# Low query parts laid out twice for the attention scores, and the meta keys' value block padded to 128 rows

## Chip, cores and metric

The kernel runs on one core of a Trainium2 chip. The metric is device time in microseconds (us) of one execution of the whole program; lower is better. In the profile PE is TensorE's matmuls, PEld its weight loads, DVE is VectorE, ACT is ScalarE, POOL is GpSimd and SP the queue that issues most DMAs.

## What is computed

One decoder layer. 16 learned meta tokens stand ahead of 1024 input tokens, so attention has 1040 key positions. Reduced to what matters here:

```python
hn = rms_norm(h, norm1_gain);  proj = hn @ w_in             # q, k, v and the conv input
q, k = rms_norm(q), rms_norm(k)                             # 4 heads x 2 components x 64
q, k = apply_partial_rope(q), apply_partial_rope(k)
s = einsum('bqhcd,bkhcd->bhcqk', q, k) * scale              # two score maps per head
p = softmax(where(mask, s, -inf))                           # causal
a = p[:, :, 0] - lam * p[:, :, 1]                           # differential attention
o = einsum('bhqk,bkhe->bqhe', a, v)                         # value width 128
h = h + concat(rms_norm(o) * 0.8, conv_branch(u)) @ w_out
h = h + relu(rms_norm(h) @ w_up) ** 2 @ w_down
return h[:, 16:]
```

Model width is 1024, feed-forward width 4096, everything float32.

## The kernel before, in words

Float32 products are made from two-part numbers: a high part that TensorE's reduced float32 format (fp32r) holds exactly, and a low part, the rest. The helper `split` (lines 119 to 121) makes both: ScalarE copies to the high part (L120), VectorE, or GpSimd on request, subtracts it for the low part (L121). A product is then high x high + high x low + low x high, the three matmuls of `three` (L311 to L313).

The stages follow one another: norm and transposes of x, projections for the conv branch, k, q and v (to about 285 us, the last ones mixed with the first attention work), attention with the conv half and part of the attention half of the output projection set in between (to about 506 us), the rest of the projection with the second norm, and the feed-forward part (from about 540 us).

Attention goes over 32 units (i, h): query tile i from 7 down to 0, head h from 0 to 3. Tile i sees 16 + 128 (i + 1) keys, so units get smaller. For each unit:

- `qstack` (L496 to L513) lays out the 128 queries of head h: for both components c a high part of 64 columns, written twice side by side (`qt_dup`, by ScalarE at L503, by VectorE at L505 for i of 0 and 1), and a low part written once (`qt_lo`, L506; by VectorE for i above 3, by GpSimd for i up to 3). Three 128x128 transposes (L510) turn it into a PSUM bank, and one ScalarE copy (L512) brings it to the tile `uq`, whose ring has 3 buffers (UQB). In `uq` slots 0 and 1 have the high part of component c on all 128 rows (twice 64); slot 2 has the low part of component 0 on rows 0 to 63 and that of component 1 on rows 64 to 127.
- `scores` (L515 to L583) multiplies with the keys. The key tile `kst` has for each component the high part of k on one half of the 128 rows and the low part on the other half; the order of the halves is such that the high part of component c lies on rows 64c to 64c + 63. Line L532 contracts 128 rows, high q with high and low k; line L533 adds low q with high k, and contracts 64 rows. A causal mask is added to the last 128 columns by a bf16 matmul (L535). A unit's keys come in one or two pieces of at most 512 columns per component; for i = 7 the 16 meta keys are a piece of their own, in the fourth part of the query bank.
- The rest of `scores` takes a row maximum on VectorE (L572 or L542) and the exponential with its sum on ScalarE (L576 or L546); score tiles have two buffers.
- `mix` (L585 to L605) combines the two components on VectorE (L591), transposes the result in blocks of 128 keys, four to a PSUM bank (L602), and splits it into `u` (L120, L121). Block 0 is the 16 meta keys; where the number of blocks is one more than a multiple of four (i = 7 and 3) it has a bank of its own, 16 rows high.
- `values` (L607 to L621) multiplies `u` with the values, two matmuls per block (L616, L617). For block 0 both contract 16 rows, with the tile `vm` (16 rows) as the other operand.

Query layouts are issued three units ahead of `mix`, scores two ahead (LOOK). Values follow one unit behind. At given units the output projection's matmuls (`po`, from `conv_out` and `attn_out`) are put in at another priority. All instructions of an engine run in an order fixed at build time: `TileContext` is told to lay it out by priorities and a planner's own estimate of durations, so an edit can move the order of work that it doesn't touch. The PSUM ring `x` (2 banks) is shared by query transposes, `values` and `po`.

Of the kernel before, what the change touches and what calls it, by code (L numbers as in the profile page):

```python
# [9 lines left out]
F32 = mybir.dt.float32  # L10
F32R = mybir.dt.float32r
BF16 = mybir.dt.bfloat16
AF = mybir.ActivationFunctionType
# [3 lines left out]
P = 128  # L17
# [12 lines left out]
LOOK = 2  # L30
UQB = 3
FIN = 3
# [21 lines left out]
def hybrid_layer_kernel(  # L54
# [40 lines left out]
    RS = G  # L95
# [1 line left out]
    warm = cp.tile([P, 1], F32, tag="warm", name="warm")  # L97
# [14 lines left out]
    def rsqrt_of(dst, ss, eps):  # L112
        """dst = (ss + eps) ** -0.5"""
        parts, n = ss.shape
        ms = small([P, 8], "ms", 4)[:parts, :n]
        RS.tensor_scalar(ms, ss, eps, None, ALU.add)
        G.tensor_tensor(out=dst, in0=ms, in1=mhalf[:parts, :n], op=ALU.pow)
# [32 lines left out]

# [1 line left out]
    # the meta tokens: high parts in columns 0..15, low parts in columns 32..47  # L152
    xm = cp.tile([P, 8, 48], F32R, tag="xm", name="xm")
# [16 lines left out]
    def norm_tile(src, parts, dst, t=-1):  # L170
        """src [parts, D] -> src * rstd * norm1, transposed and split by dst(half, bank)."""
        ss = small([P, 1], "ss")
        junk = sp.tile([P, D], BF16, tag="tmp", name="junk", bufs=4)
        S.activation(junk[:parts, :], src, AF.Square, accum_out=ss[:parts])
        rs = small([P, 1], "rs")
        rsqrt_of(rs[:parts], ss[:parts], D * EPS)
        V.tensor_scalar(src, src, rs[:parts, 0:1], D ** 0.5, ALU.mult, ALU.mult)
        for hf in range(2):
            bank = pa.tile([P, 4, P], F32, tag="mm", name="xtr") if t in XPA else tr_bank("xtr")
            for q in range(4):  # L180
                k = hf * 4 + q
                T.transpose(bank[:, q, :parts], src[:, k * P:(k + 1) * P], ident[:parts, :parts])
            dst(hf, bank)
# [26 lines left out]

    # small parameters
    cvec = cp.tile([P, 4, 4], F32, tag="cvec", name="cvec")
# [43 lines left out]

# [1 line left out]
    NK = NPOS // 2  # L258
# [7 lines left out]
    def fir(dst, src, k0, tap, n, bias, ka, kb):  # L266
        """dst[k - k0] = bias + sum_d tap(d) src[k - d], k = ka .. kb - 1"""
        if bias is None:
            S.activation(dst[:, ka - k0:kb - k0], src[:, ka:kb], AF.Copy, scale=tap(0))
        else:  # L270
            S.activation(dst[:, ka - k0:kb - k0], src[:, ka:kb], AF.Identity, bias=bias, scale=tap(0))
        for d in range(1, n):
            lo = max(ka, d)
            o = dst[:, lo - k0:kb - k0]
            V.scalar_tensor_tensor(o, src[:, lo - d:kb - d], tap(d), o, ALU.mult, ALU.add)
# [3 lines left out]
    def conv_taps(j, ka, kb, which):  # L279
        """31 taps as three filters of half the length: on the even, the odd and the summed positions."""  # L280
        hb = yt[:, j, :].rearrange("p (s k) -> p s k", s=2)
# [27 lines left out]
    def three(ps, st, mv, first, last):  # L309
        """ps += st_hi*mv_hi + st_hi*mv_lo + st_lo*mv_hi"""  # L310
        T.matmul(ps, st[0], mv[0], start=first, stop=False)  # L311
        T.matmul(ps, st[0], mv[1], start=False, stop=False)  # L312
        T.matmul(ps, st[1], mv[0], start=False, stop=last)  # L313
# [27 lines left out]

# [1 line left out]
    def proj(w, t, bank=None):  # L343
        """tokens of tile t (None: meta) times the 512 columns of w."""
        if bank is None:
            bank = pa.tile([P, 512], F32, tag="mm", name="pq")
        if t is None:
            # rows 0..15: the high parts of the meta tokens, rows 32..47: the low parts
            for k in range(8):
                wk = w[k // 4]  # L350
                for part in range(2):
                    T.matmul(bank[:48, :], xm[:, k, :], wk[:, part, k % 4, :],
                             start=k == 0 and part == 0, stop=k == 7 and part == 1)
            both = tmp([P, 512], F32, "pm")[:NMETA, :]
            S.activation(both, bank[32:32 + NMETA, :], AF.Copy)
            V.tensor_tensor(out=both, in0=both, in1=bank[:NMETA, :], op=ALU.add)
            return both
        for k in range(8):
            c0 = xcol(t)
            st = (xT[t // 2][:, 0, k, c0:c0 + P], xT[t // 2][:, 1, k, c0:c0 + P])  # L360
            wk = w[k // 4]
            three(bank, st, (wk[:, 0, k % 4, :], wk[:, 1, k % 4, :]), k == 0, k == 7)
        return bank
# [8 lines left out]
    def rope_inplace(v, tab, tt, n):  # L372
        """v [n, 8, 64]: rotates the first 16 of each 64."""
        m1 = tmp([P, 2, 8, 2, 8], F32, "rot")
# [76 lines left out]
    def conv_norm(t):  # L451
        """layer norm over the channels of tile t, token-major, in place of the conv output"""
        cs = slice(t * P, (t + 1) * P)
# [37 lines left out]

# [1 line left out]
    ma = [None, None]  # L493
    l0s = small([P, NT, NH], "l0s", bufs=1)

    def qstack(i, h, pool=None):  # L496
        qt = sp.tile([P, 384], F32R, tag="raw", name="qt", bufs=4)
        qsrc = qs[:, i, h * P:(h + 1) * P].rearrange("p (c d) -> p c d", c=2)
        qt_dup = qt[:, 0:256].rearrange("p (c b d) -> p c b d", c=2, b=2)
        qt_lo = qt[:, 256:384].rearrange("p (c d) -> p c d", c=2)  # L500
        qdup = qsrc.unsqueeze(2).broadcast_to([P, 2, 2, HD])
        if i > QDI:
            S.activation(qt_dup, qdup, AF.Copy)  # L503
        else:
            V.tensor_copy(qt_dup, qdup)  # L505
        (G if i <= QG else V).tensor_tensor(out=qt_lo, in0=qsrc, in1=qt_dup[:, :, 0, :].bitcast(F32), op=ALU.subtract)  # L506
        qtf = qt.bitcast(F32)
        bank = pb.tile([P, 4, P], F32, tag="x", name="qtr", bufs=2)
        for q in range(3):
            T.transpose(bank[:, q, :], qtf[:, q * P:(q + 1) * P], ident)  # L510
        uq = pool.tile([P, 3, P], F32R, tag=f"uq{h}", name=f"uq{h}") if pool else ap.tile([P, 3, P], F32R, tag="uq", name="uq", bufs=UQB)
        S.activation(uq, bank[:, 0:3, :], AF.Copy)  # L512
        return uq, bank  # L513

    def scores(i, h, uq, bank, pool=None):  # L515
# [12 lines left out]
        def score(ps, c, k0, k1):  # L528
            kt = kst[h // 2][:, 2 * (h % 2) + c, :]
            rows = slice(64 * c, 64 * c + 64)  # L530
            diag = k1 == nkeys
            T.matmul(ps, uq[:, c, :], kt[:, k0:k1], start=True, stop=False)  # L532
            T.matmul(ps, uq[rows, 2, :], kt[rows, k0:k1], start=False, stop=not diag)  # L533
            if diag:
                T.matmul(ps[:, k1 - k0 - P:k1 - k0], identb, maskb, start=False, stop=True)  # L535
# [49 lines left out]
    def mix(i, h, pt, l1):  # L585
# [7 lines left out]
        u = ap.tile([P, 2, 9, P], F32R, tag="u", name="u")  # L593
        merged = (i + 2) % 4 != 1
        groups = [list(range(b, min(b + 4, i + 2))) for b in range(0 if merged else 1, i + 2, 4)]
        for grp in groups if merged else [[0]] + groups:
            bank = tr_bank("atr")
            n = P if merged or grp[0] else NMETA
            for q, b in enumerate(grp):
                # of block 0 only the first NMETA keys are used  # L600
                k0 = NMETA + P * (b - 1) if b else 0
                T.transpose(bank[:n, q, :], a[:, k0:k0 + n], ident)  # L602
            b0, b1 = grp[0], grp[-1] + 1
            split(u[:n, 0, b0:b1, :], u[:n, 1, b0:b1, :], bank[:n, :b1 - b0, :])
        return u  # L605

    def values(i, h, u):  # L607
# [5 lines left out]
        for b in range(i + 2):  # L613
            n = P if b else NMETA
            vb = (vs[(b - 1) // 4][:, (b - 1) % 4] if b else vm)[:, h]
            T.matmul(ops, u[:n, 0, b, :], vb.rearrange("p a e -> p (a e)"), start=b == 0, stop=False)  # L616
            T.matmul(ops[:, 0:P], u[:n, 1, b, :], vb[:, 0, :], start=False, stop=b == i + 1)  # L617
        ob = ap.tile([P, P], F32, tag="ob", name="ob")
# [23 lines left out]

# [1 line left out]
    def wout(e, nh, rows):  # L644
# [64 lines left out]
    ap = at_pool.__enter__()  # L709
    vm = ap.tile([NMETA, NH, 2, P], F32R, tag="vm", name="vm", bufs=1)  # L710
    split(vm[:, :, 0, :], vm[:, :, 1, :], psm.rearrange("p (h e) -> p h e", h=NH))

# [57 lines left out]

# [1 line left out]
    hn = [None, None]  # L772
# [30 lines left out]

# [1 line left out]
    NB = NF // 512  # L805
# [97 lines left out]
```

## Time and profile before

| | |
|---|---|
| median of 3 runs | 1240.09 us |
| lowest and highest | 1232.40 and 1240.16 us |
| span of the profiled execution | 1236.3 us |
| median less span | 3.8 us |
| TensorE busy, share of the span | 99% |
| weight loads busy | 81% |
| VectorE busy | 55% |
| ScalarE busy | 36% |
| GpSimd busy | 10% |

The time of the profiled execution is not listed apart from its span. The span runs from the first to the last instruction; what lies around it is taken as the 3.8 us that the median is longer. TensorE's busy time is made of modelled ends: consecutive matmuls overlap in it, so the distance from one matmul's start to the next one's tells more than its duration.

### The profile page before, as it was taken

To read this page: it belongs to the slowest core of one execution; us is meant where nothing else is said; L and a number is where in the kernel's file an instruction comes from. 1 tells how busy PE (TensorE), PEld (TensorE's weight loads), DVE (VectorE), ACT (ScalarE), POOL (GpSimd) and SP (SyncE) were. 2 spreads that over 40 slices of the span, in tenths; PEclk is the share of its full clock that TensorE was granted. 3 is DMA by queue.
4 is the path that set the end of the run, shared out by engine and by line. 5 is a ranking of instruction groups with operands and counts; after the bars stand their busy time and mean duration, and the time that the engine had idled before them with its cause. 6 is when DMAs were issued, how large, how long until landed. Compare 5 with 4: busy or idle time off the path is not lost.

```text
span 1236.3 us, 15700 instructions
## 1 busy us (share of the span) xinstructions
PE 1220.1 (99%) x6048; PEld 1002.1 (81%) x6048; DVE 677.3 (55%) x1286; ACT 439.1 (36%) x1120; POOL 126.2 (10%) x143
## 2 busy tenths in 40 slices
PE   6999999999999999999999999999999999999998
PEld 6999888766777777888888888888888888888887
DVE  7699899767676667674244334324324343342322
ACT  7422556265565655653033022122221230230310
POOL 3000853130011311210000000000000000000000
PEclk9999999989999999999999999999999999999999
DMA  7320110001122401421022012102202210220112
GB/s 260 95 69 1 35 35 11 25 17 52 51 86 72 140 28 31 136 74 44 25 68 68 8 61 68 51 19 68 69 1 68 68 39 30 69 68 1 34 43 94
DMA packets 37979, 70.64 MB, mean 57 GB/s; under 512 B 4864, under 2 KB 5120, under 8 KB 37904
## 3 DMA queue, kind: packets, MB, share of 16 engines
q1 hardware_dynamic: 37904, 69.64, 17.5%
q8 instruction: 47, 0.77, 0.3%
q14 instruction: 28, 0.23, 0.1%
HBM read 61.23 MB, written 8.39 MB: 56 GB/s over the span
## 4 chain that ended last, share of the span: by engine, by line
PE 96%; issue 2%; DVE 1%; POOL 1%; DMA 0%; ACT 0%; SPq 0%; POOLq 0%; DVEq 0%
PE pf L311 9%; PE pf L312 9%; PE pd L313 9%; PE pf L313 9%; PE pd L312 9%; PE pd L311 9%; PE ops L616 3%; PE sps L533 3%; PE pu L311 3%; PE pu L313 2%; PE pu L312 2%; PE po L311 2%; PE pq L312 2%; PE pq L311 2%; PE pq L313 2%; PE po L313 2%
## 5 line engine op out<-in xcount | busy, mean ns | idle before, releaser
L846 DVE TENSOR_TENSOR h<-h,pd 128x512 f32<-128x512 f32 x128 | 87.9, 687 | 205.5 <-PE pd L313 205.5
L312 PE MATMUL pf<-hn,wup 128*128 128x512 f32 x512 | 199.5, 390 | 0.0
L311 PE MATMUL pd<-wdn,at 128*128 128x512 f32 x512 | 199.2, 389 | 0.0
L312 PE MATMUL pd<-wdn,at 128*128 128x512 f32 x512 | 199.2, 389 | 0.0
L313 PE MATMUL pd<-wdn,at 128*128 128x512 f32 x512 | 199.2, 389 | 0.0
L313 PE MATMUL pf<-hn,wup 128*128 128x512 f32 x512 | 199.1, 389 | 0.0
L311 PE MATMUL pf<-hn,wup 128*128 128x512 f32 x512 | 198.4, 390 | 0.7 <-ACT hn L120 0.7
L831 DVE TENSOR_TENSOR r<-r 128x512 f32<-128x512 f32 x64 | 44.3, 691 | 162.9 <-ACT r L830 162.9
L120 ACT ACTIVATE wdn<-raw 128x512 fp32r<-128x512 f32 x64 | 37.8, 626 | 268.0 <-PE pd L313 246.8
L311 PEld LDWEIGHTS pf<-hn,wup 128*128 128x128 f32 x512 | 96.0, 188 | 20.8 <-ACT hn L120 1.0
L312 PEld LDWEIGHTS pd<-wdn,at 128*128 128x128 f32 x512 | 96.1, 188 | 20.0
L311 PEld LDWEIGHTS pd<-wdn,at 128*128 128x128 f32 x512 | 96.1, 188 | 19.9
L313 PEld LDWEIGHTS pd<-wdn,at 128*128 128x128 f32 x512 | 96.1, 188 | 19.9
L313 PEld LDWEIGHTS pf<-hn,wup 128*128 128x128 f32 x512 | 96.1, 188 | 19.8
L312 PEld LDWEIGHTS pf<-hn,wup 128*128 128x128 f32 x512 | 96.1, 188 | 19.8
L830 ACT ACTIVATE r<-pf 128x512 f32<-128x512 f32 x64 | 38.2, 597 | 169.8 <-PE pf L313 169.0
L312 PE MATMUL pu<-xT,w 128*128 128x260 f32 x256 | 72.2, 285 | 0.0
L313 PE MATMUL pu<-xT,w 128*128 128x260 f32 x256 | 71.5, 284 | 0.0
L311 PE MATMUL pu<-xT,w 128*128 128x260 f32 x256 | 71.5, 285 | 0.0
L121 DVE TENSOR_TENSOR at<-r,at 128x512 fp32r<-128x512 f32 x64 | 44.3, 692 | 37.8 <-ACT at L120 37.7
L120 ACT ACTIVATE at<-r 128x512 fp32r<-128x512 f32 x64 | 40.3, 630 | 41.6 <-DVE r L831 41.6
L131 DVE SCALAR_TENSOR_TENSOR wup<-raw,gains,wup 128x512 fp32r<-128x512 f32 x64 | 45.3, 748 | 15.6 <-ACT wup L130 14.5
(218 smaller groups left out, 2227.8 us busy)
## 6 DMA issues: line engine op xcount, KB each, us to landing
raw<-in_w_up SPq DMA_DIRECT2D x64, 256.0 KB, 3.3
raw<-in_w_down SPq DMA_DIRECT2D x64, 256.0 KB, 3.0
raw<-in_w_in SPq DMA_DIRECT2D x40, 256.0 KB, 2.9
xs<-in_x SPq DMA_DIRECT2D x8, 512.0 KB, 6.5
raw<-in_w_out SPq DMA_DIRECT2D x16, 256.0 KB, 2.9
xr<-in_x SPq DMA_DIRECT2D x16, 256.0 KB, 2.7
cvo<-cvo SPq DMA_DIRECT2D x16, 256.0 KB, 2.1
h<-cvo SPq DMA_DIRECT2D x16, 256.0 KB, 5.2
```

The costliest lines, as they stand in the source:

```text
L120: S.activation(hi, src, AF.Copy)
L121: (eng or V).tensor_tensor(out=lo, in0=src, in1=hi.bitcast(F32), op=ALU.subtract)
L131: V.scalar_tensor_tensor(w[:, 1, k, :], raw, g, w[:, 0, k, :].bitcast(F32), ALU.mult, ALU.subtract)
L311: T.matmul(ps, st[0], mv[0], start=first, stop=False)
L312: T.matmul(ps, st[0], mv[1], start=False, stop=False)
L313: T.matmul(ps, st[1], mv[0], start=False, stop=last)
L533: T.matmul(ps, uq[rows, 2, :], kt[rows, k0:k1], start=False, stop=not diag)
L616: T.matmul(ops, u[:n, 0, b, :], vb.rearrange("p a e -> p (a e)"), start=b == 0, stop=False)
L830: S.activation(r, ps, AF.Relu)
L831: V.tensor_tensor(out=r, in0=r, in1=r, op=ALU.mult)
L846: V.tensor_tensor(out=hs, in0=hs, in1=ps, op=ALU.add)
```

## The change

The low part of the queries is written twice too, like the high part. `uq` gets four slots in place of three: slot 2 + c has the low part of component c on all 128 rows. Line L533 then contracts 128 rows: low q with high and low k, which adds the product low x low that was left out before. A query layout has four transposes, its low part and its copy are wider, and the ring of `uq` has two buffers.

The tile `vm` gets 128 rows, cleared by a GpSimd memset; the meta values stay in rows 0 to 15. Block 0 of `mix` is transposed and split at full height everywhere, so that its rows 16 to 127 hold other keys' weights, which meet the zero rows of `vm`. The partly filled bank of `mix` comes first in place of last, so for i = 5 the groups are 3 and 4 blocks (before 4 and 3), and for i = 4 they are 2 and 4 (before 4 and 2).

```diff
-UQB = 3
+UQB = 2
...
     def qstack(i, h, pool=None):
-        qt = sp.tile([P, 384], F32R, tag="raw", name="qt", bufs=4)
+        qt = sp.tile([P, 2, 2, 2, HD], F32R, tag="raw", name="qt", bufs=4)
...
-        qt_dup = qt[:, 0:256].rearrange("p (c b d) -> p c b d", c=2, b=2)
-        qt_lo = qt[:, 256:384].rearrange("p (c d) -> p c d", c=2)
+        qt_dup, qt_lo = qt[:, 0], qt[:, 1]
...
-        (G if i <= QG else V).tensor_tensor(out=qt_lo, in0=qsrc, in1=qt_dup[:, :, 0, :].bitcast(F32), op=ALU.subtract)
-        qtf = qt.bitcast(F32)
+        (G if i <= QG else V).tensor_tensor(out=qt_lo, in0=qdup, in1=qt_dup.bitcast(F32), op=ALU.subtract)
+        qtf = qt.bitcast(F32).rearrange("p a c b d -> p (a c b d)")
...
-        for q in range(3):
+        for q in range(4):
             T.transpose(bank[:, q, :], qtf[:, q * P:(q + 1) * P], ident)
-        uq = pool.tile([P, 3, P], F32R, tag=f"uq{h}", name=f"uq{h}") if pool else ap.tile([P, 3, P], F32R, tag="uq", name="uq", bufs=UQB)
-        S.activation(uq, bank[:, 0:3, :], AF.Copy)
+        uq = pool.tile([P, 4, P], F32R, tag=f"uq{h}", name=f"uq{h}") if pool else ap.tile([P, 4, P], F32R, tag="uq", name="uq", bufs=UQB)
+        S.activation(uq, bank, AF.Copy)
...
-            T.matmul(ps, uq[rows, 2, :], kt[rows, k0:k1], start=False, stop=not diag)
+            T.matmul(ps, uq[:, 2 + c, :], kt[:, k0:k1], start=False, stop=not diag)
...
-        merged = (i + 2) % 4 != 1
-        groups = [list(range(b, min(b + 4, i + 2))) for b in range(0 if merged else 1, i + 2, 4)]
-        for grp in groups if merged else [[0]] + groups:
+        first = (i + 2) % 4 or 4
+        groups = [list(range(first))] + [list(range(b, b + 4)) for b in range(first, i + 2, 4)]
+        for grp in groups:
...
-                T.transpose(bank[:n, q, :], a[:, k0:k0 + n], ident)
+                T.transpose(bank[:, q, :], a[:, k0:k0 + P], ident)
             b0, b1 = grp[0], grp[-1] + 1
-            split(u[:n, 0, b0:b1, :], u[:n, 1, b0:b1, :], bank[:n, :b1 - b0, :])
+            split(u[:, 0, b0:b1, :], u[:, 1, b0:b1, :], bank[:, :b1 - b0, :])
...
-            n = P if b else NMETA
             vb = (vs[(b - 1) // 4][:, (b - 1) % 4] if b else vm)[:, h]
-            T.matmul(ops, u[:n, 0, b, :], vb.rearrange("p a e -> p (a e)"), start=b == 0, stop=False)
-            T.matmul(ops[:, 0:P], u[:n, 1, b, :], vb[:, 0, :], start=False, stop=b == i + 1)
+            T.matmul(ops, u[:, 0, b, :], vb.rearrange("p a e -> p (a e)"), start=b == 0, stop=False)
+            T.matmul(ops[:, 0:P], u[:, 1, b, :], vb[:, 0, :], start=False, stop=b == i + 1)
...
-    vm = ap.tile([NMETA, NH, 2, P], F32R, tag="vm", name="vm", bufs=1)
-    split(vm[:, :, 0, :], vm[:, :, 1, :], psm.rearrange("p (h e) -> p h e", h=NH))
+    vm = ap.tile([P, NH, 2, P], F32R, tag="vm", name="vm", bufs=1)
+    G.memset(vm.bitcast(F32), 0.0)
+    split(vm[:NMETA, :, 0, :], vm[:NMETA, :, 1, :], psm.rearrange("p (h e) -> p h e", h=NH))
```

The rest of the diff takes out comments.

## Rows read from the trace of the kernel before

**Rows 1.** Busy time by stretch: us (xinstructions) per engine, granted clock, DMA share, GB/s.

```profile
...
285.00:300.00 15.00, 14.20 (x69) 9.60 (x66) 11.54 (x28) 10.24 (x23) 0.00 (x0) 1.00 0.22 70
285.00:506.00 221.00, 219.82 (x1192) 164.74 (x1190) 152.61 (x382) 128.49 (x355) 33.34 (x42) 0.99 0.20 65
540.00:1236.00 696.00, 692.67 (x3069) 573.33 (x3067) 258.98 (x386) 156.63 (x257) 0.79 (x2) 1.00 0.16 50
...
```

**Rows 2.** The view of cores: span and mean granted TensorE clock.

```profile
...
core 0: 1236.3 us, clock 0.996
...
```

**Rows 3.** Timeline from 315.8 us: start us, us, engine, line, tiles, form [idle before].

```profile
...
315.85 0.49 ACT L512 ACTIVATE uq<-qtr 128x384 fp32r<-128x384 f32 x1
...
316.27 0.18 PEld L533 LDWEIGHTS sps<-kst,uq 64*128 64x128 f32 x1 [0.22 <-issue]
...
316.68 0.23 PE L535 MATMUL sps<-maskb,identb 128*128 128x128 bf16 x1
...
316.84 0.38 PE L616 MATMUL ops<-vm,u 16*128 16x256 f32 x1
...
317.06 0.22 PE L617 MATMUL ops<-vm,u 16*128 16x128 f32 x1
...
317.21 0.39 PE L616 MATMUL ops<-vs,u 128*128 128x256 f32 x1
...
317.43 0.19 PEld L616 LDWEIGHTS ops<-vs,u 128*128 128x128 f32 x1
317.49 0.33 PE L616 MATMUL ops<-vs,u 128*128 128x256 f32 x1
...
317.72 0.33 PE L616 MATMUL ops<-vs,u 128*128 128x256 f32 x1
...
318.18 0.42 PE L532 MATMUL sps<-kst,uq 128*128 128x456 f32 x1
...
318.53 0.47 PE L533 MATMUL sps<-kst,uq 64*128 64x456 f32 x1
...
318.93 0.48 PE L532 MATMUL sps<-kst,uq 128*128 128x456 f32 x1
...
319.34 0.47 PE L533 MATMUL sps<-kst,uq 64*128 64x456 f32 x1
...
319.74 0.23 PE L535 MATMUL sps<-maskb,identb 128*128 128x128 bf16 x1
...
319.77 0.36 PE L616 MATMUL ops<-vs,u 128*128 128x256 f32 x1
...
```

**Rows 4.** The score tile's view: L533's matmuls, and its engine's idle time.

```profile
...
L533 PE MATMUL sps<-kst,uq x104: 330/438/792, 245.9 to 495.7; 64*128 64x512 f32 x16, 64*128 64x456 f32 x16, 64*128 64x392 f32 x16, 64*128 64x328 f32 x16
...
  issue: 23.0, 105
...
```

**Rows 5.** Timeline from 433.3 us: the end of unit (3, 2)'s scores.

```profile
...
433.30 0.39 PE L532 MATMUL sps<-kst,uq 128*128 128x264 f32 x1
...
433.62 0.38 PE L533 MATMUL sps<-kst,uq 64*128 64x264 f32 x1
...
433.93 0.23 PE L535 MATMUL sps<-maskb,identb 128*128 128x128 bf16 x1
...
```

**Rows 6.** Timeline of TensorE at 278.2 us: eight 128x128 transposes.

```profile
...
278.22 1.03 PE L480 MATMUL ctr<-ident,yt 128*128 128x128 f32 x8
...
```

**Rows 7.** Groups by line and form: busy us, mean ns | idle before, releaser.

```profile
...
L506 DVE TENSOR_TENSOR qt<-qs,qt 128x128 fp32r<-128x128 f32 x16 | 5.6, 349 | 1.7 <-ACT qt L503 1.7
...
L512 ACT ACTIVATE uq<-qtr 128x384 fp32r<-128x384 f32 x32 | 15.7, 489 | 21.3 <-PE qtr L510 21.2
...
L506 POOL TENSOR_TENSOR qt<-qs,qt 128x128 fp32r<-128x128 f32 x16 | 8.4, 527 | 32.0 <-DVE qt L505 22.4 <-ACT qt L503 9.6
L154 POOL MEMSET xm<- 128x384 f32 x1 | 0.4, 418 | 0.0
...
```

**Rows 8.** Timeline at 439.1 us: the query copy of unit (2, 0).

```profile
...
439.13 0.49 ACT L512 ACTIVATE uq<-qtr 128x384 fp32r<-128x384 f32 x1 [0.97 <-PE qtr L510]
...
```

More of the change, by code (lines that the diff above doesn't have):

```diff
@@ L529, in score @@
             kt = kst[h // 2][:, 2 * (h % 2) + c, :]
-            rows = slice(64 * c, 64 * c + 64)
             diag = k1 == nkeys
             T.matmul(ps, uq[:, c, :], kt[:, k0:k1], start=True, stop=False)
-            T.matmul(ps, uq[rows, 2, :], kt[rows, k0:k1], start=False, stop=not diag)
+            T.matmul(ps, uq[:, 2 + c, :], kt[:, k0:k1], start=False, stop=not diag)
             if diag:
@@ L593, in mix @@
         u = ap.tile([P, 2, 9, P], F32R, tag="u", name="u")
-        merged = (i + 2) % 4 != 1
-        groups = [list(range(b, min(b + 4, i + 2))) for b in range(0 if merged else 1, i + 2, 4)]
-        for grp in groups if merged else [[0]] + groups:
+        first = (i + 2) % 4 or 4
+        groups = [list(range(first))] + [list(range(b, b + 4)) for b in range(first, i + 2, 4)]
+        for grp in groups:
             bank = tr_bank("atr")
-            n = P if merged or grp[0] else NMETA
             for q, b in enumerate(grp):
                 k0 = NMETA + P * (b - 1) if b else 0
-                T.transpose(bank[:n, q, :], a[:, k0:k0 + n], ident)
+                T.transpose(bank[:, q, :], a[:, k0:k0 + P], ident)
             b0, b1 = grp[0], grp[-1] + 1
-            split(u[:n, 0, b0:b1, :], u[:n, 1, b0:b1, :], bank[:n, :b1 - b0, :])
+            split(u[:, 0, b0:b1, :], u[:, 1, b0:b1, :], bank[:, :b1 - b0, :])
         return u
```

## Prediction

> **What bounds the kernel now.** I read the stretches first, then the timeline inside attention, then the view of the score tile. By stretch [rows 1], TensorE is busy for 219.8 of the 221 us from 285 to 506, where nearly all of attention lies, and for 692.7 of the 696 us of the feed-forward stage; VectorE is at 69% of the attention stretch and ScalarE at 58%. So TensorE sets the end, and it hardly waits for anybody. But its busy time counts overlapping, modelled ends, and hides what a matmul really takes from the next one. The yardstick for that is the feed-forward stage: 3069 matmuls, nearly all 512 wide over 128 rows, in 696 us, hence 0.227 us from start to start.
>
> The timeline in attention [rows 3] doesn't keep that pace. A 456-wide matmul should take 0.227 x 456/512 = 0.20 us. The one over 64 rows (L533) takes 0.40 (318.53 to 318.93, and 319.34 to 319.74), and the 128-row one (L532) 0.41 where it follows a 64-row matmul (318.93 to 319.34) and 0.35 where it follows a 128-row one (318.18 to 318.53). The reason can be seen in the weight loads. That of L533 starts at 316.27 after 0.22 us in which the load port was idle and nothing was waited for ("issue"), whereas the load of the 128-row value matmul at 317.49 begins at 317.43, when a 128-row matmul before it has just started. So between matmuls of equal height the load is hidden behind the previous matmul, and at each change of height it stands open. The score tile's view has 105 such gaps with 23.0 us in all [rows 4], 0.22 each. At 264 columns [rows 5] starts are 0.32 and 0.31 apart against 0.12 by the yardstick: the loss of some 0.20 us doesn't depend on the width.
>
> Here the Trainium skill speaks against the change. Its page "TensorE: Matmul & The Clock Gate", section "Part 3: Packing small matmuls", says that a weight load overlaps with matmuls in flight only when its row group differs; on that, matmuls that all use 128 rows would hide nothing. Its page "TensorEngine Tiling (Array Packing)", section "Key Properties", says instead that changing the tiling mode drains the engine. The rows above (317.43 against 317.49 for equal heights, 0.22 us of idle at a change) agree with the second; what the first would give is a rival below.
>
> **The change part by part.** *Scores.* There are 104 pairs of L532 and L533 on the score tile [rows 4], and 8 more for the 16 meta keys of i = 7 (four heads, two components). After the change both matmuls of a pair are 128 rows high, like the hidden case. L533 loses 0.40 - 0.20 = 0.20. L532 loses 0.21 or 0.15; both orders occur, and I take the middle, 0.18. That is 0.38 per pair. The 8 pairs of 144 columns (i = 0) and the 8 of 16 columns have no row here; I charge them half, between nothing and the full price. So 96 x 0.38 + 16 x 0.19 = 39.5 us, bounds 36.5 and 42.6.
>
> *Meta keys' values.* The step into the 16-row matmul takes 0.16 after L535 (316.68 to 316.84) against 0.03 into a 128-row one (319.74 to 319.77), and the 16-row pair 0.37 (316.84 to 317.21) against 0.23 for a 128-row pair (317.49 to 317.72) [rows 3]. That is 0.13 + 0.14 = 0.27 for each of 32 units, 8.6 us. Where a transpose and not L535 goes before, the first part could be smaller: without it, 4.5 us.
>
> *Added on TensorE.* One more transpose per unit. Eight of them take 1.03 us with the last one's tail [rows 6], 0.13 each, so 32 x 0.13 = 4.2 us, all on the path. The 8 transposes of block 0 for i = 7 and 3 get 128 stationary columns in place of 16; they stream the same 128 columns, so I take nothing, at most 8 x 0.13 = 1.0.
>
> *Added on the other engines* [rows 7]. The low part doubles from 128 to 256 columns: at most another 0.349 us on VectorE for 16 units (5.6 us) and another 0.527 on GpSimd for 16 (8.4 us). The copy to `uq` grows by a third: 0.489 to at most 0.652, 32 times, 5.2 us on ScalarE. The memset of `vm`, 128x1024, is by proportion to the 0.418 us of a 128x384 one some 1.1 us. It can start when the weights of v are done with, at the end of the stage before, and is needed by the first `values`; GpSimd does nothing from 285 to 300 [rows 1], so the attention work that TensorE has in that time covers it. Without that cover the first `values` would wait for 1.1 us, once.
>
> *The ring of two.* The copy to `uq` of unit n now waits for the scores of unit n - 2, where it waited for n - 3. Queued behind it on ScalarE are exponentials, and its PSUM bank is one of the two of ring `x`. For unit (2, 0) the copy starts at 439.13 [rows 8] and the scores two units back ended at 434.2 [rows 5]: 5 us of slack. The closest is unit (6, 2), copied at 315.85 while the scores of (6, 0) end at 316.7 [rows 3]: 0.9 us late. I take nothing, at most a microsecond or two.
>
> *What is late next.* TensorE's own sum is -39.5 - 8.6 + 4.2 = -43.9 us. Some 4 us of it lie before 285 (the 12 pairs of the first two units, four of them 16 wide: 8 x 0.38 + 4 x 0.19 = 3.8), 40 in the stretch of 221, which would shrink to 181. VectorE would then need 152.6 + 5.6 = 158.2 of it, 87%, ScalarE 133.7, 74%. No engine is over its time, but VectorE has little left, and its maxima, subtractions and sums stand in the loops that free score banks. The row nearest to that state is 285 to 300: VectorE at 77%, ScalarE at 68%, and TensorE idle for 0.8 of 15 us, 5.3%. I charge that share of 181, 9.7 us, less the 1.2 that is idle already: +8.5. The planner may lay out the order anew; from the rows this can be worth the idle time that is there now (-1.2) or another such share (+9.7). I take nothing.
>
> *The clock.* The mean granted clock is 0.996 [rows 2], so about 5.1 us are now lost to the lower of its two levels, 1.2 GHz in place of 2.4. Fewer idle loads might end that (-5.1), new waits might add as much. I take nothing.
>
> **The sum.** The span goes from 1236.3 to 1236.3 - 43.9 + 8.5 = 1200.9; with the 3.8 us by which the median is longer, 1204.7, so 1205 us.
>
> **The rivals.** *A: VectorE becomes the bound and half the gain goes.* If VectorE can't be filled beyond the 77% of 285 to 300, the stretch takes 158.2 / 0.77 = 205.5 us, 15.5 less than now; with the 3.8 us before it the time is 1221. For it: each score bank needs a maximum before it can be freed, and there are two. Against: today's idle time of TensorE is small although VectorE and ScalarE wait for one another, since scores run two units ahead.
>
> *B: nothing is gained.* The loads would stay open between equal heights, because they use the same rows. Then only the added transposes count: 1240.1 + 4.2 = 1244. Against it are the value pairs at 0.23 us and the load at 317.43 [rows 3]. The rule of the Trainium skill's page "TensorE: Matmul & The Clock Gate" named above would make it so. This is also the case in which the change doesn't do what it says.
>
> *C: the ring of two ties query layout to scores, and the kernel is slower.* Place: the copy at L512, ahead of exponentials in ScalarE's order. If each of 30 units made TensorE wait, the 43.9 us are eaten from 1.5 us per unit on; at 2 us the time is 1240.1 - 43.9 + 60 = 1256. For it is the one unit with the negative slack; against it the 5 us elsewhere, and that the scores, too, end earlier.
>
> **How the numbers follow.** Chances: forecast 0.70, A 0.21, B 0.05, C 0.04. A measurement of this kernel can tell about 1% (12.4 us) from no change: below 1227.7 is faster, above 1252.5 slower. Forecast and A are faster (0.91), B is the same (0.05), C slower (0.04). The range: at the low end no new waits and no time at the low clock, 1240.1 - 43.9 - 1.2 - 5.1 = 1190, taken as 1191; at the high end A with a late microsecond of the ring, 1222. B, C and the forecast's tails are left out.
>
> **What would show it.** In the profile after, L533 at 128 rows with its load starting ahead of its matmul, the idle time "issue" of the score tile near zero, and 456-wide starts 0.20 apart confirm the scores; a step of about 0.03 into L616 of `vm` and 0.23 for its pair confirm the values; four transposes in one query group are 0.13 dearer. VectorE at 80% or more between 285 us and the end of attention, with TensorE waiting for maxima or for ScalarE's copies, shows the part that I charge with 8.5. The prediction is wrong if loads stay open between 128-row matmuls, if TensorE's idle time in attention passes 20 us, or if copies to `uq` are released by scores.

## The result and the profile after

The changed kernel takes 1200.43 us (median of 4 runs, 1200.07 to 1201.42), against 1239.23 us before (4 runs, 1232.40 to 1240.16). The ratio is 0.9706, 95% interval 0.9665 to 0.9746: about 39 us or 3% faster, where 1205 was forecast.

The profiled execution took 1200.07 us; its span is 1198.3. So 1.8 us lie around the span, and not the 3.8 that the forecast took from the median. With 1.8, the execution profiled before took 1238.1.

The page's first part of the kernel after:

```profile
span 1198.3 us, 15772 instructions
...
PE 1177.3 (98%) x6080; PEld 994.3 (83%) x6080; DVE 680.6 (57%) x1286; ACT 442.4 (37%) x1120; POOL 128.2 (11%) x144
...
```

The view of cores, with the mean granted clock:

```profile
...
core 0: 1198.3 us, clock 1.000
...
```

It answers to [rows 2]: no time at the lower clock, where before a mean of 0.996 cost about 5 us. The stretch of attention, by the columns of [rows 1]; it ends at about 468 us in place of 506:

```profile
...
285.00:468.00 183.00, 179.14 (x1196) 155.62 (x1195) 151.31 (x373) 126.35 (x344) 38.15 (x42) 1.00 0.24 78
...
```

TensorE is busy for 179.1 of 183 us, VectorE for 151.3 (83%), ScalarE for 126.4 (69%). TensorE still sets the end, but it now stands idle for 3.9 us in this stretch where it was 1.2.

The timeline shows a group of scores after the change; lines L532, L533 and L535 of before are L530, L531 and L533 here. It answers to [rows 3]:

```profile
...
298.54 0.39 PE L531 MATMUL sps<-kst,uq 128*128 128x512 f32 x1
...
298.77 0.23 PE L533 MATMUL sps<-maskb,identb 128*128 128x128 bf16 x1
...
298.81 0.48 PE L313 MATMUL po<-wo,mc 128*128 128x512 f32 x1
...
299.13 0.37 PE L530 MATMUL sps<-kst,uq 128*128 128x456 f32 x1
...
299.33 0.37 PE L531 MATMUL sps<-kst,uq 128*128 128x456 f32 x1
299.33 0.19 PEld L530 LDWEIGHTS sps<-kst,uq 128*128 128x128 f32 x1
299.54 0.37 PE L530 MATMUL sps<-kst,uq 128*128 128x456 f32 x1
...
299.75 0.37 PE L531 MATMUL sps<-kst,uq 128*128 128x456 f32 x1
299.96 0.10 PEld L533 LDWEIGHTS <-identb 128*128 128x128 bf16 x1 [0.23 <-issue]
299.96 0.23 PE L533 MATMUL sps<-maskb,identb 128*128 128x128 bf16 x1
...
```

Starts of 456-wide matmuls are now 0.20 to 0.21 us apart (299.13, 299.33, 299.54, 299.75, 299.96), where they were 0.35 to 0.41. The load of the matmul at 299.54 begins at 299.33, when the matmul before it starts: it is hidden. Two more things are to be seen. The mask's load still shows 0.23 us of idle load port, but the step to it is no longer than the others: an idle load port alone isn't a cost, only a late start is. And the step after a mask is short, 0.04 (298.77 to 298.81), but the matmul behind it pays for that: 0.32 us (298.81 to 299.13) at 512 columns, where the pace is 0.227.

The meta keys' values (L612 and L613 with `vm`, L616 and L617 before):

```profile
...
308.57 0.19 PEld L612 LDWEIGHTS ops<-vm,u 128*128 128x128 f32 x1
308.60 0.36 PE L612 MATMUL ops<-vm,u 128*128 128x256 f32 x1
...
308.81 0.22 PE L613 MATMUL ops<-vm,u 128*128 128x128 f32 x1
...
308.86 0.33 PE L612 MATMUL ops<-vs,u 128*128 128x256 f32 x1
...
309.09 0.33 PE L612 MATMUL ops<-vs,u 128*128 128x256 f32 x1
...
```

The pair takes 0.26 us (308.60 to 308.86) against 0.37, its neighbour 0.23. The score tile's view, with what ended the idle time of the engines that work on the tile (us, times):

```profile
...
L531 PE MATMUL sps<-kst,uq x104: 272/336/425, 245.4 to 458.8; 128*128 128x512 f32 x16, 128*128 128x456 f32 x16, 128*128 128x392 f32 x16, 128*128 128x328 f32 x16
...
  DVE bias L573: 7.2, 8
  PE sps L533: 3.1, 5
  DVE bias L542: 0.7, 2
  ACT pt L544: 0.3, 1
...
```

The entry "issue" of [rows 4] (23.0 us, 105 times) is gone. The groups of the other engines, by the columns of [rows 7]; first VectorE:

```profile
...
L505 DVE TENSOR_TENSOR qt<-qs,qt 128x256 fp32r<-128x256 f32 x16 | 8.2, 512 | 1.2 <-ACT qt L502 1.2
...
```

ScalarE:

```profile
...
L511 ACT ACTIVATE uq<-qtr 128x512 fp32r<-128x512 f32 x32 | 19.2, 599 | 6.5 <-PE qtr L509 6.4
...
```

GpSimd:

```profile
...
L505 POOL TENSOR_TENSOR qt<-qs,qt 128x256 fp32r<-128x256 f32 x16 | 13.4, 843 | 23.8 <-DVE qt L504 8.9 <-ACT qt L502 7.0 <-DVE bias L542 6.4
...
L707 POOL MEMSET vm<- 128x1024 f32 x1 | 1.0, 954 | 8.8 <-PE pv L352 8.8
...
```

The copies to `uq` are still released by the transposes (L509) and not by scores, so the ring of two isn't felt. The memset took 0.95 us.

**The account.** I summed TensorE's distances from start to start over attention, from the first query transpose to the last value matmul, by the kind of the first of the two; idle time beyond the earlier matmul's end and the loss at the lower clock are kept apart. This is my own sum from the records of the two traces, in us:

```
                                          before   after   change
high-part scores (L532 / L530)              36.4    22.5    -13.9
low-part scores (L533 / L531)               38.7    19.0    -19.7
pair on the meta block                      11.8     8.4     -3.4
steps into the meta block, all kinds         6.5     3.0     -3.5
other value matmuls                         34.9    33.3     -1.6
query transposes                             9.8    13.3     +3.5
transposes in mix                           16.0    16.8     +0.8
output projection, masks, rest             100.2   100.7     +0.5
TensorE idle                                 2.5     7.3     +4.8
lost at the lower clock                      5.1     0.0     -5.1
stretch                                    262.0   224.3    -37.7
```

### The profile page after: what moved, and what is told of

Read it like the earlier page. It is cut to its first block, busy times and chain, and to the rows that moved or that the text cites. A ratio compares the mean times of both kernels' runs of the same rounds, so it can differ in the third digit from the quotient of the medians.

```text
span 1198.3 us, 15772 instructions
## 1 busy us (share of the span) xinstructions
PE 1177.3 (98%) x6080; PEld 994.3 (83%) x6080; DVE 680.6 (57%) x1286; ACT 442.4 (37%) x1120; POOL 128.2 (11%) x144
## 4 chain that ended last, share of the span: by engine, by line
PE 94%; DVE 3%; ACT 1%; issue 1%; POOL 0%; DMA 0%; SPq 0%; DVEq 0%; POOLq 0%; ACTq 0%
PE pf L311 10%; PE pf L313 10%; PE pf L312 10%; PE pd L311 10%; PE pd L312 10%; PE pd L313 10%; PE pu L311 3%; PE pu L313 3%; PE pu L312 3%; PE pq L312 2%; PE pq L311 2%; PE pq L313 2%; PE ops L612 2%; PE po L311 2%; PE po L312 2%; PE po L313 2%
## 5 line engine op out<-in xcount | busy, mean ns | idle before, releaser
L827 ACT ACTIVATE r<-pf 128x512 f32<-128x512 f32 x64 | 38.2, 597 | 170.3 <-PE pf L313 169.5
```

The source lines that it names most:

```text
L827: S.activation(r, ps, AF.Relu)
```

## The experiments

My theory: each change of row height on TensorE leaves one weight load open, some 0.2 us, and the time follows TensorE's sum of starts plus its waits. Rivals: the heights don't matter and the gain is one of order or clock; a low matmul is slow by itself; VectorE has become the bound; the ring of two ties layouts to scores. Times are medians of five or more runs beside runs of the kernel before on the same chip.

**One half of the change at a time.** Scores only: the meta block goes back to 16 rows.

```diff
-    vm = ap.tile([P, NH, 2, P], F32R, tag="vm", name="vm", bufs=1)
-    G.memset(vm.bitcast(F32), 0.0)
+    vm = ap.tile([NMETA, NH, 2, P], F32R, tag="vm", name="vm", bufs=1)
...
+            n = P if b else NMETA
...
-            T.matmul(ops, u[:, 0, b, :], vb.rearrange("p a e -> p (a e)"), start=b == 0, stop=False)
-            T.matmul(ops[:, 0:P], u[:, 1, b, :], vb[:, 0, :], start=False, stop=b == i + 1)
+            T.matmul(ops, u[:n, 0, b, :], vb.rearrange("p a e -> p (a e)"), start=b == 0, stop=False)
+            T.matmul(ops[:, 0:P], u[:n, 1, b, :], vb[:, 0, :], start=False, stop=b == i + 1)
```

> The changed kernel with the meta keys' value block back at 16 rows (the 16-row matmuls contract 16 rows again; scores stay at 128 rows). Theory (each change of row height on TensorE leaves one weight load open, about 0.2 us for the scores, 0.27 us per unit for the meta block): 1200.4 + 4.5 to 8.6 = 1205 to 1209. Rival (the gain came from the clock or from a new order of work and not from the heights): no ordered difference, 1200 within 3 us.

Measured: 1209.60 us (1208.28 to 1210.12), ratio to before 0.9774 (0.9747 to 0.9800): just above the theory's range, and clear of the rival's 1200.

Values only: the kernel before with the padded block.

```diff
-    vm = ap.tile([NMETA, NH, 2, P], F32R, tag="vm", name="vm", bufs=1)
+    vm = ap.tile([P, NH, 2, P], F32R, tag="vm", name="vm", bufs=1)
+    G.memset(vm.bitcast(F32), 0.0)
...
-            n = P if merged or grp[0] else NMETA
+            n = P
...
-            n = P if b else NMETA
+            n = P
```

> The kernel before with only the meta keys' value block padded to 128 rows. Theory: 1239.2 less 4.5 to 8.6 = 1231 to 1235. Rival (heights don't matter): 1239.

Measured: 1227.38 us (1223.81 to 1228.23), ratio 0.9920 (0.9894 to 0.9947). The kernel before had a median of 1237.58 on that chip. So the padding brings 10.2 us by itself and 9.2 on top of the scores (1209.6 - 1200.4, from two sets of runs), the scores 28.0: the two halves add up to 38.2, about the whole change. Both times lie outside the theory's ranges, by 0.6 and by some 4 us, both on the side of a padding that brings more than I had allowed. The clock comes into it (below).

**Grouping, with nothing added.** The kernel before, with the matmuls of a component ordered by height. Low parts stay on 64 rows, query layouts at three transposes.

```diff
-        def score(ps, c, k0, k1):
...
-            T.matmul(ps, uq[:, c, :], kt[:, k0:k1], start=True, stop=False)
-            T.matmul(ps, uq[rows, 2, :], kt[rows, k0:k1], start=False, stop=not diag)
+        def score(*pieces):
+            for step in (high, low, mask):
+                for piece in pieces:
+                    step(*piece)
...
-                score(sps[:, base:512], c, lead, lead + hfw)
-                score(sps[:, 512:512 + hfw], c, lead + hfw, nkeys)
+                score((sps[:, base:512], c, lead, lead + hfw), (sps[:, 512:512 + hfw], c, lead + hfw, nkeys))
```

> The kernel before, low part on 64 rows as before, but all high-part matmuls of a component (for small tiles of both components) first, then all low-part ones, then the masks. Nothing is added or removed; the changes of row height fall from four to two per component for i of 3 and more (40 times) and per unit for the 12 smaller units: 104 fewer. Theory (a change of height costs 0.19): -20 us, 1219; if moving from rows 0 to 63 to rows 64 to 127 costs as much as a change of height, 12 of them come back: 1222. Rival (a load beside a 64-row matmul is never hidden, whatever follows): only one open load in four goes, -10, 1229. Rival (128 rows are faster by themselves): no change, 1239.

Measured: 1212.82 us (1211.84 to 1215.28), ratio 0.9803 (0.9776 to 0.9830): 24.8 us faster than the 1237.58 beside it, more than the 20 of the theory. The score tile's idle entry falls from 105 gaps to this:

```profile
...
  issue: 10.2, 37
...
```

By the same account as above, high-part scores take 26.7 us in place of 36.4 and low-part scores 27.4 in place of 38.7: 21.0 us less for 104 changes of height fewer, 0.20 each. Between runs at full clock the gain is 20.3 us as well (means of 1232.76 and 1212.43); the rest of the 24.8 is the clock. The same matmuls on the same rows got cheaper by their order alone. So it isn't the 128 rows by themselves that bring the gain, and most of the price lies in the change of height. A part stays with the 64 rows, though:

```profile
...
318.74 0.37 PE L529 MATMUL sps<-kst,uq 128*128 128x456 f32 x1
319.04 0.29 PEld L534 LDWEIGHTS sps<-kst,uq 64*128 64x128 f32 x2 [0.31 <-issue]
319.04 0.68 PE L534 MATMUL sps<-kst,uq 64*128 64x456 f32 x2
...
319.65 0.23 PE L538 MATMUL sps<-maskb,identb 128*128 128x128 bf16 x1
...
```

The two low matmuls of a component, both on the same 64 rows, take 0.61 us here (319.04 to 319.65), where two at the pace would take 0.40. In the records of all 40 such pairs the second starts 0.11 us later than the pace allows, at every width (0.31 after the first at 456 columns). So a load between two 64-row matmuls on the same rows is not wholly hidden, which the rival had said in part; these 4.4 us are left in the grouped kernel and not in the changed one.

**The ring alone.** The kernel before with two buffers.

```diff
-UQB = 3
+UQB = 2
```

> The kernel before with only the ring of the query tiles cut from three buffers to two. Theory: nothing, 1239 within 3 us. Rival (the ring ties layouts to scores): 5 to 60 us slower, and copies to uq released by scores.

Measured: 1236.83 us (12 runs), ratio 0.9994 (0.9971 to 1.0018). The ring costs nothing. The other direction, the changed kernel with three buffers, wasn't run.

**How near VectorE is.** The changed kernel without its low-part score matmuls:

```diff
-            T.matmul(ps, uq[:, c, :], kt[:, k0:k1], start=True, stop=False)
-            T.matmul(ps, uq[:, 2 + c, :], kt[:, k0:k1], start=False, stop=not diag)
+            T.matmul(ps, uq[:, c, :], kt[:, k0:k1], start=True, stop=not diag)
```

> The changed kernel without the low-part score matmuls (the products of low q with k are left out; layouts, transposes and all other work stay). Theory (TensorE's own sum sets the time, VectorE has room left): the 112 matmuls' 19 us go, 1200.4 - 19 = 1181, up to 1189 if waits take nearly half. Rival (VectorE is the bound after the change): TensorE waits in their place, 1192 to 1200.

Measured: 1191.12 us (1189.19 to 1192.17), ratio 0.9623 (0.9598 to 0.9648). Of the 19 us taken from TensorE only 9 arrive (11 between runs at full clock: 1200.13 on the mean, and a single one at 1189.19): worse than the theory's range and better than the rival's end at 1192. Its attention stretch:

```profile
...
285.00:459.00 174.00, 166.99 (x1095) 143.23 (x1096) 150.07 (x372) 127.69 (x348) 37.45 (x42) 0.98 0.24 82
...
```

VectorE is at 86% (150.1 of 174), TensorE idle for 7.0 us where it was 3.9. In the account of its whole attention TensorE's idle time is 12.0 us (7.3 after the change) and 3.4 are lost at the lower clock, which was granted from 284.3 to 291.1, after TensorE had stood idle for 0.8 us at 281.4, 0.65 at 282.5 and 0.15 at 283.8; these two are 8 of the missing 10 us. Its list of waits (who waited for whom: us in total, times, longest) shows many small ones, on VectorE and on ScalarE:

```profile
...
PE atr L598 <- DVE pt L588: 1.2, 2, 0.6
...
PE ops L611 <- ACT u L120: 1.1, 1, 1.1
PE ops L611 <- ACT uq L511: 1.0, 2, 0.6
...
PE atr L598 <- DVE u L121: 1.0, 1, 1.0
...
```

So VectorE isn't a wall at the changed kernel, but of these next microseconds taken from TensorE only about half arrived.

More work for VectorE, all of the low parts:

```diff
-QG = 3
+QG = -1
```

> The changed kernel with the low parts of i up to 3 made by VectorE in place of GpSimd: 16 subtractions of 0.42 us, 6.7 us more on VectorE in the second half of attention. Theory (VectorE has room): 1200 to 1202. Rival (VectorE is the bound): 1205 to 1208.

Measured: 1200.37 us (1199.93 to 1203.07): nothing, though VectorE's busy time between 365 and 468 us rose from 82.2 to 85.5 us, from 80% to 83%. Less work for it, in the first half:

```diff
-QG = 3
+QG = 5
```

> The changed kernel with the low parts of i of 4 and 5 made by GpSimd: 8 subtractions of 0.42 us less on VectorE, 0.74 us each more on GpSimd. Theory: 1199 to 1201. Rival (VectorE is the bound): 1196 to 1197, faster than the changed kernel.

Measured: 1198.81 us (1198.43 to 1199.18), ratio to before 0.9687 (0.9659 to 0.9715). The changed kernel took 1199.41 to 1201.08 when it was run again, in another set of runs; the two ranges don't meet, but they are not from one chip, so the 1.4 us between the medians aren't shown to come from the edit. The median lies just below the theory's range and short of the rival's. Nor do the traces show a VectorE that is in the way while the tiles are large: in the changed kernel TensorE stands idle for 0.3 us between 285 and 365, and for 3.5 between 365 and 468, where this edit takes nothing from VectorE (rows under "Waits" below). This is the fastest version that I have with the whole computation.

**Grouping together with the padding**, three transposes as before, ring of two:

> The kernel before with the score matmuls grouped by height (high parts, low parts on 64 rows, masks), the value block padded to 128 rows and the ring of two; query layout with three transposes as before. Theory (costs of height changes add up): 1212.8 less the 10.2 that the padding alone brought = 1203, two or three us behind the changed kernel since two changes of height per component stay, against one transpose per unit saved. Rival (what is left comes back as waits on VectorE): 1207 and more.

Measured: 1204.43 us (1203.46 to 1207.08), ratio 0.9736 (0.9710 to 0.9762). The costs add up as the theory says. All but 4 of the 39 us are to be had without a fourth transpose or a wider low part, by order and padding.

**Both components side by side**, on top of that. The same, with for i from 3 to 6:

```diff
+            for c in range(2):
+                both[c] = pb.tile([P, 1024], F32, tag="s", name="sps")
+            hfw = nmain // 2
+            score(*[(both[c][:, b:b + hfw], c, k, k + hfw)
+                    for b, k in ((512 - hfw, 0), (512, hfw)) for c in range(2)])
```

> The grouped kernel with the padded value block and the ring of two, and for i from 6 to 3 also both components of a unit together: four high-part matmuls, then the low parts of both components in turn (rows 0 to 63, rows 64 to 127), then the masks. In the grouped runs two low parts on different rows started 0.003 us apart. Theory (matmuls on different halves of the rows run at the same time, and a unit keeps only two changes of height): TensorE needs 16 x 0.8 = 13 us less than the grouped kernel with padded values at 1204.4, 3 us less than the changed kernel, and one transpose per unit fewer: 1192 to 1198 if waits don't grow. Rival (the second half of the rows has to wait where both write for long): no gain, 1204. Rival (both score buffers held at once cost the overlap with maxima and exponentials): waits of 0.5 us or more per unit, 1200 to 1210.

Measured: 1204.18 us (1203.37 to 1204.90). It is a miss, and it tells neither theory nor rivals apart: the timeline of TensorE shows that the planner kept the components apart, high and low of one, then of the other, as without the edit.

```profile
...
315.15 0.63 PE L529 MATMUL sps<-kst,uq 128*128 128x456 f32 x2
315.71 0.68 PE L534 MATMUL sps<-kst,uq 64*128 64x456 f32 x2
316.33 0.23 PE L538 MATMUL sps<-maskb,identb 128*128 128x128 bf16 x1
...
316.65 0.67 PE L529 MATMUL sps<-kst,uq 128*128 128x456 f32 x2
317.25 0.67 PE L534 MATMUL sps<-kst,uq 64*128 64x456 f32 x2
...
```

> The same with the low parts of i of 4 and 5 made by GpSimd. Theory (TensorE's sum sets the time): within 2 us of the one without. Rival (VectorE has become the bound): 2 to 4 us faster.

Measured: 1204.60 us (1203.74 to 1204.78). Moving the low parts to GpSimd does nothing here, where VectorE has 80% of the stretch. The changed kernel beside these two:

> The changed kernel beside these two on the same chip: 1200.4 within 1.

Measured: 1200.18 us (1199.41 to 1201.08), ratio 0.9708 (0.9683 to 0.9733).

## Why the prediction was right

**What bounds the kernel** was read rightly: taking work from TensorE alone moved the time, and grouping showed that the open loads were the work.

**Scores: right in kind, too large.** The forecast took 39.5 us from the two lines, with 36.5 as its lower bound; the account gives 33.6 (13.9 + 19.7), outside the bounds. The step that was mis-sized is the pace that it assumed for what is left: 0.227 us per 512 columns, by width alone. That holds inside a run of scores (0.20 to 0.21 at 456), but not behind a mask or a transpose, where the step before is short; the 0.32 us at 298.81 is such a place. In the records a high-part matmul after the change takes 0.005 us more than the pace behind a low-part one, but 0.09 more behind a mask (27 times) or a transpose (20 times). Before the change this extra stood in one number with the open load behind it, 0.18 behind a mask, and the forecast put all of it down to the height. Most of the error is in the high-part line: 18.7 us were forecast for it and 13.9 came.

**Meta keys' values: right in total, by some luck.** 8.6 us were forecast, 4.5 for the pair and 4.1 for the step into it; the account gives 3.4 + 3.5, and 1.6 more for the other value matmuls, 8.5 together. The forecast had nothing for these 1.6, but they belong to the padding: in the values-only kernel the other value matmuls fall from 34.9 to 33.3 as well. The padding by itself measured 10.2 with the clock in it. That transposes and not masks often go before didn't lower the price: the usual step into the block fell from 0.20 to 0.03 behind a transpose and from 0.16 to 0.04 behind a mask.

**The added transposes: right in total.** 4.2 us were forecast; the query transposes took 3.5 more (0.13 each counts the last one's tail; start to start they are 0.11 apart), and those of `mix` 0.8 more. The 8 full transposes of block 0 cost nothing, as forecast: in the values-only kernel, which has them too, the transposes of `mix` take 16.1 us against 16.0.

**The other engines: bounds held.** The low part cost VectorE 0.512 us on average against a bound of 0.698, the copy to `uq` 0.599 against 0.652, GpSimd 0.843 against 1.054, the memset 0.954 against an estimate of 1.1, hidden as said. VectorE's share is 83%. The forecast's 87 left out its own 8.5 us of waits; with them 158.2 of 189.5 us is 83% as well.

**Waits: too dear, and not those that were named.** 8.5 us were charged for the stretch from 285 us on; TensorE's idle time rose by 4.8 in all attention and by 2.7 in that stretch. The waits of the stretch after the change:

```profile
...
PEld L533 <- issue: 5.1, 26, 0.3
...
PE qtr L509 <- DVE msb L555: 1.7, 1, 1.7
...
PE atr L599 <- DVE sr L628: 0.8, 1, 0.8
...
PE ops L612 <- DVE osb L616: 0.8, 2, 0.5
...
```

The first line is the masks' loads, whose idle port was seen above to cost nothing. The waits of TensorE's matmuls are all for VectorE, the longest one 1.7 us: for copies, sums, products and splits, and none for a maximum or for ScalarE's copies to `uq`, which the prediction had named as the sign. The two parts of the stretch, by the columns of [rows 1]:

```profile
...
285.00:365.00 80.00, 79.67 (x523) 69.24 (x521) 69.07 (x156) 53.69 (x127) 7.65 (x8) 1.00 0.25 82
365.00:468.00 103.00, 99.46 (x676) 86.38 (x675) 82.24 (x218) 72.66 (x217) 30.50 (x34) 1.00 0.22 76
...
```

TensorE is idle for 0.3 us where VectorE has 86%, and for 3.5 where it has 80%. So VectorE's share doesn't foretell the waits here, which the forecast had taken from a row with a high share.

Rival A, that VectorE can't be filled beyond 77%, is refuted by the 83% that it reaches, and the 86% from 285 to 365. Waits for other engines do eat a further gain, though: one more cut on TensorE of 19 us gave back about half.

**The clock: taken at nothing, it is worth about 5 us in these medians.** Runs list their granted clock. Among the 17 runs of the kernel before that stood beside the first experiments five at 1.000 take 1232.64 to 1232.86 us, five at 0.996 take 1236.57 to 1238.16, five at 0.994 take 1239.92 to 1240.60, the one at 0.998 takes 1235.08 and the one at 0.991 takes 1242.87. The changed kernel's ten runs are at 0.997 (two), 0.999 (one) and 1.000 (seven). So from full clock to full clock the change is worth 32.6 us (means of 1232.76 and 1200.13), and the rest of the 39 between the medians is time that TensorE no longer spends at the lower level. That fewer open loads keep the clock up fits all kernels here in which changes of height were cut (their runs are at 0.997 or above), but the kernel before has runs at 1.000 too, and what lets the clock fall was not tested by itself.

**The sum.** With these sizes: -33.6 - 8.5 + 4.3 + 0.5 + 4.8 - 5.1 = -37.6, and 1238.1 - 37.6 = 1200.5, where the profiled execution took 1200.07. The forecast's errors partly cancelled: scores too large by 6, waits too dear by 4, clock missed by 5, the time around the span too long by 2. That it came within 5 us owes something to luck; what was right is the mechanism, that changes of row height leave loads open.

Rival B is refuted twice, by the load at 299.33 that begins beside a matmul of equal height, and by the grouped kernel. Here the trace differs from what the Trainium skill says on the page "TensorE: Matmul & The Clock Gate", section "Part 3: Packing small matmuls", that loads overlap with running matmuls only if the row group differs: the measurement decides. Rival C is refuted by the ring alone, ratio 0.9994.

## What to carry to other kernels

Look at the distance from one matmul's start to the next beside that of the best stage of the same kernel: TensorE was 99% busy here, and equal row heights took off a sixth of the attention stage (42 of 262 us) that it had lost to open weight loads. Where heights must differ, order the matmuls by height first, since that adds no work and brought 25 of the 39 us (20 of 33 between runs at full clock), and pad to full height where the group is too small to order. Price what is left from rows with the same neighbours, since a full-height matmul behind a short step took 0.09 us more than its width says. Expect part of a further gain to be lost to waits for other engines, about half of 19 us here; the next engine's share of busy time didn't tell where they come.

## What the runs showed of the hardware that I had not expected

In the grouped kernel the small units put a low matmul on rows 0 to 63 right before one on rows 64 to 127. The timeline merges such neighbours (x2):

```profile
...
429.61 0.53 PE L529 MATMUL sps<-kst,uq 128*128 128x400 f32 x2
...
430.06 0.19 PEld L534 LDWEIGHTS sps<-kst,uq 64*128 64x128 f32 x2 [0.27 <-issue]
430.07 0.45 PE L534 MATMUL sps<-kst,uq 64*128 64x400 f32 x2
...
430.45 0.28 PE L538 MATMUL sps<-maskb,identb 128*128 128x128 bf16 x2
...
```

The two 400-wide low matmuls together take 0.38 us to the mask behind them (430.07 to 430.45), with one open load in it, where two after one another at the pace would need 2 x 0.18 and the open load. In the records of all 12 such units the second starts 0.003 to 0.004 us after the first. So matmuls on different halves of the rows ran at the same time. The Trainium skill's page "TensorE: Matmul & The Clock Gate", section "Part 3: Packing small matmuls", has it so, with about 4 ns between starts; the trace agrees. Two low matmuls on the same 64 rows in a two-piece unit are 0.31 us apart at 456 columns, which is slower than full-height ones (0.20 to 0.21). Whether this could be used for the large units stays open, since the planner kept their components apart.

The second is how evenly the time follows the granted clock: the runs of one and the same program lie at a few levels, 1232.8, 1236 to 1238, 1240 and 1243 us, by mean clocks of 1.000, 0.996, 0.994 and 0.991. A gain of half a per cent can't be read from such runs without looking at their clock.
